# A two-layer hybrid diffusion block on one core: the second layer's modulation sums in the context feed-forward, norm scaling of queries and keys on ScalarE, mean squares of the latents by TensorE and one GpSimd power

## The chip, the cores and the metric

The kernel runs on one core of a Trainium2 chip, in one launch. The metric is the device time of one execution in microseconds (us), as the median of several. The engines are named as the profile does: PE (TensorE), PEld (its weight loads), DVE (VectorE), ACT (ScalarE), POOL (GpSimd) and SP, on whose queue all DMAs here are issued. Each engine executes its instructions in the order of its own stream.

## What is computed

A batch of one with 1024 latent tokens `x` and 256 context tokens `ctx`, width 1024, goes through two layers. Each layer has a mixer (layer 0 recurrent, layer 1 grouped-query attention with 8 query and 2 key heads of 128) and a gated feed-forward of 2816 with a convolution over tokens. Both are fed by a root-mean-square norm that is modulated by six vectors, which come from the condition `c` (for latents) or `c_ctx` (for context) by a product with `mod_w`:

```python
ml = _ada(c, mod_w[i], mod_b[i])          # six vectors of 1024: silu(c) @ w + b
mc = _ada(c_ctx[None], mod_w[i], mod_b[i])
h_l = _modulate(_rms(x), ml[0], ml[1])    # rms(x) * (1 + ml[1]) + ml[0]
...
x = x + ml[2] * mix_l
x = x + ml[5] * _conv_ffn(_modulate(_rms(x), ml[3], ml[4]), ffn_w_up[i], ffn_conv[i], ffn_w_down[i])
# _rms(x) = x * rsqrt(mean(x*x) + EPS)
# layer 1, queries and keys of each head: q = _rms(q) * q_norm; then a rotation (latents only)
```

The context's own output in layer 1 is not needed: there it gives keys and values only, so of `mc` of layer 1 just the shift and the scale of the mixer's input (indices 0 and 1) are used. The result is `_rms(x) * final_norm`.

## The kernel before

The latents are held transposed (features on partitions, tokens along the free axis) in two chunks of 512, `xT[1]` and `xT[2]`, and the context in `xT[0]`. Matmuls that matter for accuracy run as three passes over numbers split into a high and a low part (`mm3`, L155 to L157, with `split` at L160). A scheduler that simulates all engines sets the order of each engine's stream from the program's order, so moving code also moves the order of neighbouring instructions.

The stages, with their places in the profiled execution: the recurrent mixer of layer 0 (to 1020 us); its output projection `po` (L1292, 1020 to 1163 us), with the modulation vectors 0, 1 and 2 of layer 1 computed beside it; the context's feed-forward, `ffn_ctx` with its 22 steps of 128 features (`fg` L1206, `fd` L1215), beside which `ffn_prep` makes the latents' feed-forward input in pieces of 128 tokens (1163 to 1400 us); the latents' feed-forward of layer 0 (to 2105 us); the projections to values, keys and queries (2105 to 2325 us); attention and its output projection `apo` (to 2742 us), beside whose end `ffn_prep` runs again, for layer 1; the latents' feed-forward of layer 1 (to 3440 us); the last norm.

A modulation vector is made by `mod_steps`: for each of 8 blocks of 128 features a DMA loads a row block `mw` of `mod_w`, DVE multiplies it by the condition's scalar per partition and adds it into `macc` (L103), and at the end matmuls with a column of ones sum `macc` over partitions (`mps`, L229). For layer 1 this runs in blocks of 1024 columns beside `po` (24 loads of 512 KB), and in half blocks of 512 columns for indices 4, 3 and 5 in the key and query loops through `fill`, two steps per block of tokens (48 loads of 256 KB).

The norm of latents (`normalised`) squares a piece on ACT, sums over the 8 feature blocks on DVE with a TENSOR_REDUCE (L169), sums over partitions with a matmul that also transposes, so that the mean squares stand one per partition (`rm_cs`), raises that column to the power -1/2 on POOL (L176, 128x1 per 128 tokens), puts it on a diagonal (`rm_dg`) and multiplies by ones to spread it over all partitions (L180). `rms_mod` uses it for the input of the projections in four pieces of 256 tokens, `ffn_prep` in eight of 128.

In the projections, `proj` makes a block of 128 tokens by 256 columns with 24 matmuls (`qps`); there are 10 blocks for values (`v_proj`), 10 for keys and 32 for queries. `norm_rope` treats each key and query block: squares on ACT (`qsq`), TENSOR_REDUCE on DVE (`qss`, L1415), the power on POOL (`qrs`, 128x2, L1418), the scaling `qn<-qps,qrs` on DVE, the rotation with a table `tab` on DVE and POOL, and transposes on PE (`ktr`, `qtr`).

## Time and profile before

| | |
|---|---|
| median of 3 runs | 3487.37 us (3487.34 to 3493.24) |
| the profiled execution's own time | 3481.7 us |
| its span, first to last instruction | 3479.9 us |
| mean granted TensorE clock | 0.959 |
| PE busy | 3199.2 us, 92% of the span |
| DVE busy | 2385.0 us, 69% |
| POOL busy | 1579.2 us, 45% |
| ACT busy | 1277.4 us, 37% |
| DMA | 350 MB, mean 101 GB/s |

An engine's busy share is an average over stages with different limits. In the rows below, "idle before" is the time in which the engine had nothing to do ahead of the instructions of that row, with what ended most of it; a timeline row gives the start, the duration, the engine, the line and the tiles (out<-in).

### The profile page before, as it was taken

Reading aid. Unit: us, or ns where it says so; the run is one execution under the profiler, and the core shown is the slowest. Engines: PE = TensorE matmul, PEld = TensorE weight load, DVE = VectorE, ACT = ScalarE, POOL = GpSimd, SP = SyncE. Lnnn points to the kernel's source line nnn. Section 1 sums busy time; section 2 is a strip of 40 time slices with the busy share of each in tenths; the row PEclk is TensorE's granted clock in tenths of the full one; section 3 lists DMA queues with packets and bytes.
Section 4 is the critical chain, followed back from the end, with each engine's and each line's share of the span. In section 5 each row is a group of like instructions: output and inputs, shape, how many; then the busy total and the mean of one; then the engine's idle time right before and its main releaser. Section 6 shows DMA issues by size and latency. Waiting matters only on the chain.

```text
span 3479.9 us, 47261 instructions
## 1 busy us (share of the span) xinstructions
PE 3199.2 (92%) x16708; PEld 2676.1 (77%) x16708; DVE 2385.0 (69%) x3991; ACT 1277.4 (37%) x2772; POOL 1579.2 (45%) x1513
## 2 busy tenths in 40 slices
PE   7877988899979999799999997989999799999998
PEld 4766867687757888688788877878888677887877
DVE  5777365768857445677767677887657777767677
ACT  4423133654332122333333323236656433333333
POOL 2364463523304111565555543653433665655554
PEclk9988999999989999899999998999999899999999
DMA  5546455555476553211111122540110111111111
GB/s 186 151 119 170 130 148 147 151 156 174 153 258 215 146 152 118 77 58 44 52 58 49 58 67 72 160 141 25 37 55 28 37 50 42 52 58 49 58 49 73
DMA packets 446154, 350.12 MB, mean 101 GB/s; under 512 B 56756, under 2 KB 392862, under 8 KB 445150
## 3 DMA queue, kind: packets, MB, share of 16 engines
q1 hardware_dynamic: 445918, 347.10, 33.2%
q8 instruction: 132, 2.16, 0.3%
q14 instruction: 104, 0.85, 0.1%
HBM read 286.25 MB, written 60.76 MB: 100 GB/s over the span
## 4 chain that ended last, share of the span: by engine, by line
PE 41%; DVE 9%; POOL 3%; issue 2%; DMA 2%; ACT 2%; DVEq 0%; SPq 0%; POOLq 0%; ACTq 0%
PE fg L157 6%; PE fg L156 6%; PE fg L155 6%; PE fd L156 4%; PE fd L157 4%; PE fd L155 4%; PE apo L155 2%; DVE st L94 2%; PE apo L157 2%; PE apo L156 2%; PE apt L1521 2%; DMA mw<-in_mod_w_dram 2%; POOL w1l L94 1%; PE s L155 1%; DVE ft L103 1%
## 5 line engine op out<-in xcount | busy, mean ns | idle before, releaser
L103 DVE SCALAR_TENSOR_TENSOR xT<-fd,mod,xT 128x512 f32<-128x512 f32 (+1 forms) x432 | 291.1, 693 | 216.9 <-PE fd L157 176.8
L155 PE MATMUL pj<-hhi,whi 128*128 128x512 f32 (+1 forms) x696 | 263.2, 378 | 21.9 <-ACT raw L510 14.1
L103 DVE SCALAR_TENSOR_TENSOR macc<-mw,sc,macc 128x256 f32<-128x256 f32 (+2 forms) x301 | 231.6, 805 | 73.3 <-DMA mw<-in_mod_w_dram 71.7
L156 PE MATMUL fd<-gl,dh 128*128 128x512 f32 (+1 forms) x688 | 267.7, 389 | 7.1 <-DVE gl L94 7.1
L157 PE MATMUL fd<-gh,dl 128*128 128x512 f32 (+1 forms) x688 | 266.8, 388 | 0.0
L155 PE MATMUL fd<-gh,dh 128*128 128x512 f32 (+1 forms) x688 | 262.5, 392 | 1.6 <-ACT gh L1143 1.4
L156 PE MATMUL pj<-hlo,whi 128*128 128x512 f32 (+1 forms) x696 | 261.0, 375 | 0.7 <-DVE hlo L94 0.7
L157 PE MATMUL pj<-hhi,wlo 128*128 128x512 f32 (+1 forms) x696 | 260.5, 374 | 0.0
L94 DVE TENSOR_TENSOR st<-st 128x512 f32<-128x512 f32 x176 | 211.8, 1203 | 52.1 <-POOL s1l L94 34.1
L100 POOL TENSOR_SCALAR P<-P,rc 128x512 f32<-128x512 f32 (+1 forms) x192 | 116.7, 627 | 200.9 <-DVE rc L1507 59.7
L94 POOL TENSOR_TENSOR dl<-sd,dh 128x256 fp32r<-128x256 f32 x168 | 157.1, 950 | 109.1 <-ACT dh L160 107.1
L155 PEld LDWEIGHTS pj<-hhi,whi 128*128 128x128 f32 x696 | 138.5, 199 | 45.9 <-ACT raw L510 15.5
L94 POOL TENSOR_TENSOR w0l<-st,w0h 128x1024 fp32r<-128x1024 f32 x44 | 106.4, 2417 | 135.6 <-ACT w0h L1088 119.6
L94 POOL TENSOR_TENSOR p<-p,u 128x512 f32<-128x512 f32 (+1 forms) x45 | 93.0, 2067 | 156.8 <-DVE u L94 156.8
L156 PEld LDWEIGHTS fd<-gl,dh 128*128 128x128 f32 x688 | 129.9, 189 | 40.1 <-DVE gl L94 13.5
L1206 PE MATMUL fg<-hx,st 128*128 128x256 f32 x704 | 157.1, 379 | 0.0
L155 PEld LDWEIGHTS fd<-gh,dh 128*128 128x128 f32 x688 | 127.8, 188 | 36.6 <-ACT gh L1143 11.7
L155 PE MATMUL fg<-ah,w0h 128*128 128x512 f32 (+1 forms) x360 | 142.3, 396 | 14.6 <-ACT w0h L1088 8.9
L103 DVE SCALAR_TENSOR_TENSOR ft<-fraw,conv_f,ft 128x1024 f32<-128x1024 f32 x88 | 136.0, 1546 | 26.1 <-ACT ft L91 25.4
L156 PEld LDWEIGHTS pj<-hlo,whi 128*128 128x128 f32 x696 | 138.6, 199 | 19.4 <-DVE hlo L94 1.1
L157 PEld LDWEIGHTS pj<-hhi,wlo 128*128 128x128 f32 x696 | 138.2, 199 | 18.7 <-issue 0.2
L157 PEld LDWEIGHTS fd<-gh,dl 128*128 128x128 f32 x688 | 130.0, 189 | 26.3
(609 smaller groups left out, 9734.5 us busy)
## 6 DMA issues: line engine op xcount, KB each, us to landing
st<-in_ffn_w_up_dram SPq DMA_DIRECT2D x88, 512.0 KB
st<-in_ffn_w_up_dram SPq DMA_DIRECT2D x88, 256.0 KB
sd<-in_ffn_w_down_dram SPq DMA_DIRECT2D x176, 128.0 KB
sh<-sh_scr SPq DMA_DIRECT2D x80, 256.0 KB
mw<-in_mod_w_dram SPq DMA_DIRECT2D x128, 128.0 KB
wst<-in_rec_w_in_dram SPq DMA_DIRECT2D x56, 256.0 KB
st<-in_rec_w_out_dram SPq DMA_DIRECT2D x24, 512.0 KB
mw<-in_mod_w_dram SPq DMA_DIRECT2D x24, 512.0 KB
```

The lines of the kernel that those rows point to most:

```text
L94: e.tensor_tensor(out=o, in0=a, in1=b, op=op)
L100: e.tensor_scalar(out=o, in0=a, scalar1=s1, scalar2=s2, op0=op0, op1=op1)
L103: e.scalar_tensor_tensor(out=o, in0=a, scalar=s, in1=b, op0=op0, op1=op1)
L155: T.matmul(ps, lhsT=wh, rhs=xh, start=first, stop=False)
L156: T.matmul(ps, lhsT=wh, rhs=xl, start=False, stop=False)
L157: T.matmul(ps, lhsT=wl, rhs=xh, start=False, stop=last)
L1206: T.matmul(ps, lhsT=h[k // 4][:, k % 4], rhs=hx[:, k], start=k == 0, stop=k == KD - 1)
L1521: T.transpose(pt_[:, b], P[:, (b0 + b) * 128:(b0 + b + 1) * 128], ident)
```

## The change

It has three parts. First, the twelve half vectors of layer 1 are computed in the context's feed-forward, in the order 1, 0, 2, 4, 3, 5, all 512 wide, five steps behind each of the 22 steps; the pool of weight tiles there has 12 buffers in place of 14, and the context's keys are made ahead of the latents' norm. Second, a new function `normalised_pe` takes the place of `normalised` for the input of the projections (now in pieces of 128 tokens, each followed at once by its value block) and for `ffn_prep` of layer 1: PE sums the squares over feature blocks and partitions with eight matmuls against a 128x128 matrix of ones, so that the sums stand alike on all partitions, and POOL raises the whole 128x128 tile to -1/2. The mean's factor is moved into the modulation scale as sqrt(1024). Third, `norm_rope` sums squares by the accumulator output of ACT, scales by ACT with a per-partition scale, and has its factor sqrt(128) in the norm weights.

```diff
+    def normalised_pe(tmp, psp, tag, xs):
+        n = xs.shape[-1]
+        sq = tmp.tile([128, KD, n], F32, tag="rm_sq", name="rm_sq", bufs=5 if tmp.name.startswith("tmpe") else 2)
+        act(sq, xs, AF.Square)
+        ps = psp.tile([128, 512], F32, tag=tag, name="rm_ps")[:, 0:n]
+        for k in range(KD):
+            T.matmul(ps, lhsT=ones, rhs=sq[:, k], start=k == 0, stop=k == KD - 1)
+        r = tmp.tile([128, n], F32, tag="rm_rs", name="rm_rs", bufs=2)
+        ts(V, r, ps, D * EPS, None, ALU.add)
+        G.tensor_tensor(out=r, in0=r, in1=nhalf.to_broadcast([128, n]), op=ALU.pow)
+        return r[:, None, :].to_broadcast([128, KD, n]), sq
...
             if idx in (1, 4):
-                ts(V, m_, m_, 1.0, None, ALU.add)
+                if l == 1 and d == 0:
+                    ts(V, m_, m_, 1.0, D ** 0.5, ALU.add, ALU.mult)
+                else:
+                    ts(V, m_, m_, 1.0, None, ALU.add)
...
-                for idx in ((0,), (1,), (2,))[ci]:
-                    mod_acc(mp, pd, "d", 1, idx, (0, 1) if idx < 2 else (0,), 0, 1024)
...
-            fa.st = pool(pf, "fsta", 14)
+            fa.st = pool(pf, "fsta", 12)
+            mp = pool(pf, "mpa", 1)
+            mods = (None for i in (1, 0, 2, 4, 3, 5) for h in range(2)
+                    for _ in mod_steps(mp, pd, "d", 1, i, (0, 1) if i < 2 else (0,), h, 512))
...
             for f in range(NF):
                 step(f)
-                for _ in range((1, 0)[0] * (f >= (1, 0)[1])):
-                    next(prep, None)
+                next(prep, None)
+                for _ in range(5):
+                    next(mods, None)
...
-                    rms_mod(tmp, pd, "d", xT[ci], 512, mcol(1, 0, 1), mcol(1, 0, 0), hh[ci], hl[ci], w=256)
-                    for b in range(4 * ci - 2, 4 * ci + 2):
-                        v_proj(b)
+                    def done(p0, ci=ci):
+                        v_proj(4 * ci - 2 + p0 // 128)
+                    rms_mod(tmp, pd, "d", xT[ci], 512, mcol(1, 0, 1), mcol(1, 0, 0), hh[ci], hl[ci], w=128,
+                            norm=normalised_pe, done=done)
...
+            ts(V, nb_, nb_, 128 ** 0.5, None, ALU.mult)
...
-                act(sq, ps, AF.Square)
-                ss = qt_.tile([128, 2], F32, tag="ss", name="qss")
-                V.tensor_reduce(out=ss, in_=sq, axis=AX.X, op=ALU.add)
-                ts(V, ss, ss, 1.0 / 128, EPS, ALU.mult, ALU.add)
-                rs = qt_.tile([128, 2], F32, tag="rs", name="qrs")
-                G.tensor_tensor(out=rs, in0=ss, in1=nhalf.to_broadcast([128, 2]), op=ALU.pow)
+                ss = qt_.tile([128, 2, 2], F32, tag="ss", name="qss")
+                for h in range(2):
+                    S.activation(out=sq[:, h], in_=ps[:, h], func=AF.Square, accum_out=ss[:, 0, h:h + 1])
+                ts(V, ss[:, 0], ss[:, 0], 128 * EPS, None, ALU.add)
+                G.tensor_tensor(out=ss[:, 1], in0=ss[:, 0], in1=nhalf.to_broadcast([128, 2]), op=ALU.pow)
                 qn = qt_.tile([128, 2, 128], F32, tag="qn", name="qn")
-                tt(V, qn, ps, rs[:, :, None].to_broadcast([128, 2, 128]), ALU.mult)
+                for h in range(2):
+                    act(qn[:, h], ps[:, h], AF.Copy, scale=ss[:, 1, h:h + 1])
...
-            g1, g2 = (ffn_prep(1, ops, tmp, ci, 128) for ci in (1, 2))
+            g1, g2 = (ffn_prep(1, ops, tmp, ci, 128, normalised_pe) for ci in (1, 2))
```

POOL at the start of the projections, before (`rm_cs` are the latents' mean squares, `qwl` the low parts of the projection weights, `rm_sq` and `qhl` the modulated latents):

```order
L176 TENSOR_TENSOR rm_cs<-rm_cs,nhalf 128x2
L94 TENSOR_TENSOR qwl<-qws,qwh 128x1024
L176 TENSOR_TENSOR rm_cs<-rm_cs,nhalf 128x2
L94 TENSOR_TENSOR qwl<-qws,qwh 128x1024
L100 TENSOR_SCALAR rm_sq<-rm_sq,mod_73 128x256 x2
L94 TENSOR_TENSOR qwl<-qws,qwh 128x1024
L100 TENSOR_SCALAR rm_sq<-rm_sq,mod_73 128x256 x2
L94 TENSOR_TENSOR qhl_17360<-rm_sq,qhh_17357 128x2x256 x2
L176 TENSOR_TENSOR rm_cs<-rm_cs,nhalf 128x2 x2
L100 TENSOR_SCALAR rm_sq<-rm_sq,mod_73 128x256 x4
L94 TENSOR_TENSOR qhl_17361<-rm_sq,qhh_17358 128x2x256 x2
L94 TENSOR_TENSOR qwl<-qws,qwh 128x1024 x2
```

With the change the same place reads:

```order
L94 TENSOR_TENSOR qwl<-qws,qwh 128x1024 x4
L1420 TENSOR_TENSOR qss<-qss,nhalf 128x2 x2
L190 TENSOR_TENSOR rm_rs<-rm_rs,nhalf 128x128 x2
L100 TENSOR_SCALAR rm_sq<-rm_sq,mod_71 128x128 x4
L94 TENSOR_TENSOR qhl_17653<-rm_sq,qhh_17650 128x2x128 x2
```

The last three of these rows come four times in a row; the fourth time and what follows it are these rows of POOL:

```order
L190 TENSOR_TENSOR rm_rs<-rm_rs,nhalf 128x128 x2
L100 TENSOR_SCALAR rm_sq<-rm_sq,mod_71 128x128 x4
L94 TENSOR_TENSOR qhl_17654<-rm_sq,qhh_17651 128x2x128 x2
L94 TENSOR_TENSOR tab<-tab,nb 128x1024 x2
L94 TENSOR_TENSOR qwl<-qws,qwh 128x1024 x2
L1420 TENSOR_TENSOR qss<-qss,nhalf 128x2 x3
```

The powers of the keys' and queries' norms (128x2) of the latents stand behind all eight wide powers, and so do the table and the next weights.

POOL around the end of the output projection of attention (`awlo` are the low parts of its weights, `w0l` to `s3l` those of the first feed-forward step), before:

```order
L176 TENSOR_TENSOR rm_cs<-rm_cs,nhalf 128x1
L94 TENSOR_TENSOR awlo<-awst,awhi 128x1024 x2
L176 TENSOR_TENSOR rm_cs<-rm_cs,nhalf 128x1
L94 TENSOR_TENSOR s0l<-st,s0h 128x512
L176 TENSOR_TENSOR rm_cs<-rm_cs,nhalf 128x1
L94 TENSOR_TENSOR s2l<-st,s2h 128x512
L100 TENSOR_SCALAR rm_sq<-rm_sq,mod_73 128x128 x2
L94 TENSOR_TENSOR s1l<-st,s1h 128x512
L94 TENSOR_TENSOR awlo<-awst,awhi 128x1024
L176 TENSOR_TENSOR rm_cs<-rm_cs,nhalf 128x1
L94 TENSOR_TENSOR s3l<-st,s3h 128x512
```

And with the change:

```order
L94 TENSOR_TENSOR awlo<-awst,awhi 128x1024 x2
L190 TENSOR_TENSOR rm_rs<-rm_rs,nhalf 128x128
L94 TENSOR_TENSOR s0l<-st,s0h 128x512
L94 TENSOR_TENSOR s2l<-st,s2h 128x512
L190 TENSOR_TENSOR rm_rs<-rm_rs,nhalf 128x128
L94 TENSOR_TENSOR awlo<-awst,awhi 128x1024 x2
L100 TENSOR_SCALAR rm_sq<-rm_sq,mod_71 128x128 x2
L190 TENSOR_TENSOR rm_rs<-rm_rs,nhalf 128x128
L94 TENSOR_TENSOR s1l<-st,s1h 128x512
L100 TENSOR_SCALAR rm_sq<-rm_sq,mod_71 128x128 x2
L190 TENSOR_TENSOR rm_rs<-rm_rs,nhalf 128x128
L94 TENSOR_TENSOR awlo<-awst,awhi 128x1024 x2
```

Four wide powers now stand among the low parts of the projection's weights, two of them ahead of the third and fourth `awlo`, all four ahead of the fifth and sixth. The other four stand behind the rows shown.

SP in the context's feed-forward, before:

```order
L84 DMA mw<-in_mod_w_dram 128x1024 x5
L84 DMA st<-in_rec_w_out_dram 128x8x128
L84 DMA st<-in_ffn_w_up_dram 128x4x128 x18
L84 DMA st<-in_ffn_w_down_dram 128x512 x8
L84 DMA st<-in_ffn_w_up_dram 128x4x128 x16
```

With the change, where the loads of `mod_w` for layer 1 alternate with those of the feed-forward's weights:

```order
L84 DMA st<-in_ffn_w_up_dram 128x4x128
L84 DMA mw<-in_mod_w_dram 128x512 x7
L84 DMA st<-in_ffn_w_up_dram 128x4x128 x6
L84 DMA st<-in_ffn_w_down_dram 128x512 x2
L84 DMA mw<-in_mod_w_dram 128x512
L84 DMA st<-in_ffn_w_down_dram 128x512
L84 DMA mw<-in_mod_w_dram 128x512
L84 DMA st<-in_ffn_w_down_dram 128x512
```

The loads of `mod_w` left the stage ahead and the projections, and stand in this queue between the weights.

## Rows read from the trace of the kernel before

**Rows 1.** The page's part 1: busy time and share of the span of each engine.
```profile
PE 3199.2 (92%) x16708; PEld 2676.1 (77%) x16708; DVE 2385.0 (69%) x3991; ACT 1277.4 (37%) x2772; POOL 1579.2 (45%) x1513
```

**Rows 2.** The table of windows: stretch, its length, busy us of each engine, clock, DMA share, GB/s.
```profile
1020.00:1163.00 143.00, 133.17 (x597) 108.62 (x597) 96.25 (x101) 32.15 (x44) 45.17 (x22) 0.96 0.72 219
1163.00:1400.00 237.00, 232.67 (x1096) 204.80 (x1095) 122.83 (x219) 57.35 (x113) 30.94 (x36) 1.00 0.46 137
2150.00:2325.00 175.00, 151.88 (x1188) 148.12 (x1186) 139.29 (x306) 41.40 (x96) 108.09 (x135) 0.95 0.55 163
```

**Rows 3.** Costliest groups, POOL: the powers (nhalf) and one elementwise product, by form.
```profile
L1603 POOL TENSOR_TENSOR zst<-zst,nhalf 128x1 f32<-128x1 f32 x8 | 4.3, 550 | 22.0 <-DVE zst L100 22.0
...
L554 POOL TENSOR_TENSOR rr<-ssq,nhalf 128x10 f32<-128x10 f32 x4 | 8.0, 1999 | 12.0 <-DVE ssq L98 11.9
...
L94 POOL TENSOR_TENSOR tab<-tab,nb 128x1024 f32<-128x1024 f32 x4 | 10.1, 2559 | 2.2 <-DMA tab<-in_rope_dram 2.2
```

**Rows 4.** One tile's view: the powers of the queries' and keys' norms (qrs), min/median/max ns.
```profile
L1418 POOL TENSOR_TENSOR qrs<-qss,nhalf x42: 690/697/1065, 2170.8 to 2323.6; 128x2 f32<-128x2 f32 x42
```

**Rows 5.** Timeline of PE and groups, 1020 to 1163: sums of the modulation products.
```profile
1111.84 3.63 PE L229 MATMUL mps<-ones,macc 128*128 128x1 f32 x32
...
L103 DVE SCALAR_TENSOR_TENSOR macc<-mw,sc,macc 128x1024 f32<-128x1024 f32 x35 | 54.0, 1578 | 12.0 <-DMA mw<-in_mod_w_dram 11.9
```

**Rows 6.** Timeline of VectorE at the end of layer 0's feed-forward; then two windows there.
```profile
2089.58 3.71 DVE L169 TENSOR_REDUCE rm_rs<-rm_sq 128x256 f32<-128x2048 f32 x1
...
2097.00:2099.80 2.80, 1.27 (x10) 1.27 (x11) 2.51 (x5) 0.00 (x0) 0.00 (x0) 1.00 0.00 0
2099.90:2103.20 3.30, 3.30 (x17) 3.30 (x17) 1.28 (x4) 0.00 (x0) 0.00 (x0) 0.50 0.00 0
```

**Rows 7.** Timeline of POOL from the start of the projections.
```profile
2105.31 0.71 POOL L176 TENSOR_TENSOR rm_cs<-rm_cs,nhalf 128x2 f32<-128x2 f32 x1 [28.16 <-DVE rm_cs L100]
...
2119.97 3.00 POOL L94 TENSOR_TENSOR qhl<-rm_sq,qhh 128x512 fp32r<-128x512 f32 x2
2132.92 1.36 POOL L176 TENSOR_TENSOR rm_cs<-rm_cs,nhalf 128x2 f32<-128x2 f32 x2 [9.95 <-DVE rm_cs L100]
...
2156.14 4.77 POOL L94 TENSOR_TENSOR qwl<-qws,qwh 128x1024 fp32r<-128x1024 f32 x2 [8.76 <-ACT qwh L160]
2161.39 4.94 POOL L94 TENSOR_TENSOR tab<-tab,nb 128x1024 f32<-128x1024 f32 x2 [0.47 <-DMA tab<-in_rope_dram]
2170.80 1.36 POOL L1418 TENSOR_TENSOR qrs<-qss,nhalf 128x2 f32<-128x2 f32 x2 [4.47 <-DVE qss L100]
```

**Rows 8.** Timeline of PE: neighbouring projection matmuls; then groups of the stretch 2105 to 2325.
```profile
2154.10 0.28 PE L155 MATMUL qps<-qwh,qhh 128*128 128x256 f32 x1
2154.22 0.28 PE L156 MATMUL qps<-qwl,qhh 128*128 128x256 f32 x1
...
L103 DVE SCALAR_TENSOR_TENSOR macc<-mw,sc,macc 128x512 f32<-128x512 f32 x42 | 40.5, 965 | 15.1 <-DMA mw<-in_mod_w_dram 14.4 <-DVE qss L1415 0.3
...
L94 DVE TENSOR_TENSOR qn<-qps,qrs 128x256 f32<-128x256 f32 x42 | 17.2, 415 | 0.6 <-POOL qrs L1418 0.5
L1415 DVE TENSOR_REDUCE qss<-qsq 128x2 f32<-128x256 f32 x42 | 17.1, 409 | 2.8 <-ACT qsq L91 2.8
...
L1454 PE MATMUL qtr<-ident,qn 128*128 128x128 f32 x60 | 12.2, 286 | 11.5 <-DVE qss L100 5.6 <-DVE qn L94 5.4 <-DVE qh L94 0.4
```

**Rows 9.** Timeline of POOL around the end of the output projection.
```profile
2701.61 4.68 POOL L94 TENSOR_TENSOR awlo<-awst,awhi 128x1024 fp32r<-128x1024 f32 x2 [0.49 <-ACT awhi L160]
2706.24 1.02 POOL L176 TENSOR_TENSOR rm_cs<-rm_cs,nhalf 128x1 f32<-128x1 f32 x1
...
2732.07 2.40 POOL L94 TENSOR_TENSOR awlo<-awst,awhi 128x1024 fp32r<-128x1024 f32 x1 [1.97 <-ACT awhi L160]
2744.70 1.58 POOL L94 TENSOR_TENSOR rm_sq<-rm_sq 128x512 f32<-128x512 f32 x1 [10.23 <-DVE rm_sq L94]
...
2789.21 2.83 POOL L94 TENSOR_TENSOR w0l<-st,w0h 128x1024 fp32r<-128x1024 f32 x1
```

More of the change, by code (lines that the diff above doesn't have):

```diff
@@ L209, in rms_mod @@
                 modulate(sq, s1, sh, hi[:, :, p0:p0 + w], lo[:, :, p0:p0 + w])
+            if done is not None:
+                done(p0)
     def mod_steps(pool, psp, tag, l, idx, conds, part, width, bufs=2):
@@ L1251 @@
             wo = pool(po, "wo", 5)
-            mp = pool(po, "mpc", 1)
             mhl = {}
@@ L1320 @@
                 step(f)
-                for _ in range((1, 0)[0] * (f >= (1, 0)[1])):
-                    next(prep, None)
+                next(prep, None)
+                for _ in range(5):
+                    next(mods, None)
             for _ in prep:
+                pass
+            for _ in mods:
                 pass
@@ L1346 @@
             hp = {i: pool(pqq, f"hQ{i}", 1, side="right") for i in (2, 1, 0)}
-            wsp = pool(pqq, "qsp", 3)
+            wsp = pool(pqq, "qsp", 4)
             wst = pool(pqq, "qst", 2)
@@ L1377, in v_proj @@
                 tt(V, vl[:, b], ps, vh[:, b].bitcast(F32), ALU.subtract)
-            for b in range(2):
-                v_proj(b)
-            with ExitStack() as pt_q:
-                tmp = pool(pt_q, "tmpq", 2, side="right")
-                for ci in (1, 2):
-                    rms_mod(tmp, pd, "d", xT[ci], 512, mcol(1, 0, 1), mcol(1, 0, 0), hh[ci], hl[ci], w=256)
-                    for b in range(4 * ci - 2, 4 * ci + 2):
-                        v_proj(b)
-            rp = pool(pqq, "rp", 1, side="right")
-            qt_ = pool(pqq, "qt", 3)
-            mq = pool(pqq, "mq", 1)
-            mods = (None for i in (4, 3, 5) for h in range(2) for _ in mod_steps(mq, pd, "d", 1, i, (0,), h, 512))
-            def fill(n):
-                for _ in range(n):
-                    next(mods, None)
-            nb_ = rp.tile([128, 2, 2, 128], F32, name="nb")
+            qt_ = pool(pqq, "qt", 3)
+            nb_ = kvp.tile([128, 2, 2, 128], F32, name="nb")
             for a, src in ((0, att_q_norm), (1, att_k_norm)):
@@ L1432, in norm_rope, with k_proj @@
                 return qn
-            LAT = range(NB)
-            load_tab(1)
-            w = load_w(1024)
-            for b in LAT:
-                fill((0,2,1)[1])
-                kn = norm_rope(proj(w, b), b, 1)
+            wk = load_w(1024)
+            def k_proj(b):
+                kn = norm_rope(proj(wk, b), b, 1)
                 pt_ = pd.tile([128, 512], F32, tag="d", name="ktr")
@@ L1445 @@
                 tt(V, kTl[:, :, b * 128:(b + 1) * 128], pv, kTh[:, :, b * 128:(b + 1) * 128].bitcast(F32), ALU.subtract)
+            for b in range(2):
+                v_proj(b)
+            for b in range(2):
+                k_proj(b)
+            with ExitStack() as pt_q:
+                tmp = pool(pt_q, "tmpq", 1, side="right")
+                for ci in (1, 2):
+                    def done(p0, ci=ci):
+                        v_proj(4 * ci - 2 + p0 // 128)
+                    rms_mod(tmp, pd, "d", xT[ci], 512, mcol(1, 0, 1), mcol(1, 0, 0), hh[ci], hl[ci], w=128,
+                            norm=normalised_pe, done=done)
+            rp = pool(pqq, "rp", 1, side="right")
+            load_tab(1)
+            for b in range(2, NB):
+                k_proj(b)
             load_tab(0)
@@ L1449 @@
                 for b in range(2, NB):
-                    fill((0,2,1)[2])
                     qn = norm_rope(proj(w, b), b, 0)
@@ L1460 @@
                         dma(aq_scr[e, 2 * u:2 * u + 2, :, (b - 2) * 128:(b - 1) * 128].rearrange("h p t -> p h t"), qh[:, e])
-            for _ in mods:
-                pass
         if dbg is not None:
```

10 lines of the change are left out of this document (4 added, 6 removed).

## The prediction

> **What bounds the kernel now.** I read the page's busy times first, then the windows of the stages that the change touches, then the costliest groups and the timelines there. PE is busy 92% of the span [rows 1], so as a rule work taken from another engine buys nothing unless PE waits for it. The windows show where PE has slack [rows 2]: in the stage of the recurrent mixer's output projection it is busy 133.17 of 143 us, in the context's feed-forward 232.67 of 237 (PE-bound, DVE only 122.83), in the projections of layer 1 151.88 of 175, with DVE at 139.29. So the projections are the one stage where DVE's load matters. They make one power of 128x2 per block, the first at 2170.8 and the last at 2323.6 us [rows 4], 42 of them: 3.7 us a block, where PE's own part is 24 matmuls that start 0.12 us apart [rows 8], 2.88 us, and two transposes.
>
> **The price that decides: a power of 128x128 on POOL.** The trace has no power that wide. It has 128x1 at 0.550 us, 128x10 at 1.999 us [rows 3] and 128x2 at 0.697 us [rows 4]. From one column to two that is 0.147 us, from one to ten (1.999 - 0.550)/9 = 0.161 us per column: the price grows by the column, and 128 columns come to 0.697 + 126 x 0.147 = 19.2 us by the one slope and 0.550 + 127 x 0.161 = 21.0 us by the other. I take 20.5 us. The bound from below is the elementwise product of 128x1024 on the same engine, 2.559 us [rows 3], 2.5 ns per column: a power at that price would take 0.55 + 127 x 0.0025 = 0.87 us. I hold to the upper pair, because those rows are the same operation with the same broadcast exponent, and three widths lie on one line. The old form needed 0.55 to 0.70 us for the same tokens, since there the mean squares stood one per partition. The change has eight wide powers in the projections and eight in the preparation of layer 1's feed-forward: 16 x 20.5 = 328 us of POOL.
>
> The Trainium skill speaks the other way: "GPSIMD Engine Reference", section 3.1 (Elementwise — side-by-side cycle accounting), gives about 2.6 cycles per element for a two-input elementwise operation, which at its 1.2 GHz would be an estimated 0.28 us for 128 columns beside the dispatch; the sum would then be that of the first rival, 3441 us. The rows above do not agree for a power: 0.147 to 0.161 us per column is some 60 times the 2.5 ns of the product.
>
> **Part by part, on the scale of the profiled execution** (3481.7 us of its own time, span 3479.9; the median of the runs shown is 3487.4, 5.7 above).
>
> *Modulation sums leave the output projection's stage.* 24 loads of 512 KB go, 12.6 MB of the 143 us x 219 GB/s = 31 MB there [rows 2], and 80 rows of `mps` on PE, of which 32 took 3.63 us [rows 5]: 9 us. PE's idle time there is 143 - 133.17 = 10 us, part of it waits for weights that queue behind these loads. DVE's 35 products (1.578 us each) [rows 5] stand beside PE's work. I take -18, between -9 (PE's rows alone) and -19 (the idle time too).
>
> *They enter the context's feed-forward.* PE gets all 128 `mps` rows: 128 x 3.63/32 = 14.5 us on an engine that is already full [rows 2]. DVE gets 128 products of 128x512 at up to 0.965 us [rows 8], up to 124 us, so 247 us against 237 + 14: just under the bound, with the first six or seven steps over it. DMA gets 25 MB in addition to 237 x 137 = 32 MB, some 230 GB/s, which is about what the stage before it does now (219). SP now issues these loads between the feed-forward's weights; what would pay there is the weight behind a waiting `mw`, and the pool still holds 12. I take +18, between +14 and +44 (the rival below).
>
> *End of layer 0's feed-forward.* Two TENSOR_REDUCE of 3.7 us each, the first at 2089.58, sit on DVE among the additions that free PE's accumulators; after the pauses the granted clock is 0.50 from 2099.9 to 2103.2, that is the lower level, where it was 1.00 before [rows 6]. Both reductions go to PE: -5, bounds -7 and 0.
>
> *The projections.* DVE loses 48 products, a reduction (0.409) and a scaling (0.415) per block [rows 8]; ACT, with 41 of 175 us [rows 2], takes the latter two at no cost, since it has over 130 us to spare. That would leave PE as the bound. But in POOL's order the eight wide powers stand ahead of the table, the next weights and every power of a latent key or query. POOL is free at about 2120 us as now (its low parts of the first piece end at 2123) [rows 7]. Powers come in pairs of 41 us, because `rm_sq` has two buffers: the squares of the next pair wait for the low parts (`qhl`) of the pair before. Between pairs stand POOL's own products and low parts, casts, the value block that PE's order places ahead of the next eight sums, and those sums; the nearest row is the present pause between pieces, 9.95 us [rows 7]. I take 9. So the latents are ready at 2121 + 4 x 41 + 4 x 9 = 2321. The table and the next weights, 4.94 + 4.77 us [rows 7], follow: 2331. Of the 40 latent key and query blocks PE has about five made by then (the accumulators it has); the other 35 cost 2.88 us and two transposes of 0.14 to 0.286 us, some 3.3 us each: 115 us. With 5 us for the chain of the last block the last power is at about 2451 in place of 2323.6: +128. Bounds: +100 (19.2 us per power, pauses of 6) and +155 (21, pauses of 13). What is late next is attention's start, and it follows at once.
>
> *The preparation of layer 1's feed-forward.* Now POOL has `awlo` at 2701.61 and 2732.07, a power of 1.02 at 2706.24, and the last `w0l` at 2789.21 [rows 9]. With the change the first wide power starts at about 2706 and ends at 2727. The low parts of two weight tiles, 2.6 us, come next; the second power ends at 2750; `awlo` twice (4.7) and a product; the third ends at 2777; the fourth at 2800; the fifth and sixth `awlo`, which PE's output projection is waiting for, end at 2805. Now they end at 2734, so attention's output projection stands still for some 70 us. Two column blocks of its matmuls, some 11 us, then finish the second chunk, and only now can the last four powers start: 2818 + 4 x 21.5 = 2904, and with the last piece's products and the first weights `w0l` at 2917 in place of 2789: +128, bounds +95 (powers of 19.2, the first two behind attention) and +140. DVE's reductions that go (2 us a piece) are covered by the powers and give nothing.
>
> **Sum:** -18 + 18 - 5 + 128 + 128 = +251, so 3481.7 + 251 = 3733, and on the scale of the median 3738 us. A measurement can tell this kernel from no change from about 0.2%, 7 us, on.
>
> **Rivals.** First, a wide power costs as an elementwise product does (0.87 us). It decides as soon as 16 powers fit into POOL's idle time, below some 3 us each. Then the projections are PE-bound: 52 blocks x 2.88 = 150, 50 pairs of transposes at 0.42 = 21, sums of squares 14, together 185 in place of 218 (2105.4 to 2323.6): -33. The preparation gives back four reductions, -8, and the rest of the terms -5: -46, 3436, on the median's scale 3441 us, faster. For it: POOL's product of 1024 columns in 2.559 us. Against it: the three widths of the power on one line. Chance 0.08. Second, the line flattens beyond ten columns, say to 10 us: nearly all 16 powers are exposed, so 16 x 10.5 less, 160 or so in the places that wait: 3578. No row speaks for it. Chance 0.06. Third, the context's feed-forward becomes DVE-bound: in the first 6.4 steps DVE has 122.83/22 + 10 x 0.965 = 15.2 us per step against PE's 10.6, 30 us in all, and if none is made up later the term is +44: 3764. For it: DVE's sum is at the bound; against it: five products a step later, and accumulators and buffers that let PE run ahead. Chance 0.13. A change that does not do what it says would be one where the wide powers stood off the path, hidden beside attention and PE; POOL's order speaks against it.
>
> **Chances.** The forecast 0.73, the third rival 0.13, the second 0.06, the first 0.08, of which 0.01 for within 0.2%. The range is the bounds of the powers and of the third rival together: low 3481.7 + 5.7 - 19 + 14 - 7 + 100 + 95 = 3670, taken at 3655 for what overlaps that I don't see; high 3764 + 27 + 12 = 3803, taken at 3815. It leaves out the first two rivals and some tails. Faster 0.07, same 0.01, slower 0.92.
>
> **What would show it.** Right: POOL's L190 group at about 20 us each, 16 of them, POOL busy some 310 us more; eight of them between 2115 and 2320 with PE mostly idle between value blocks at a low granted clock; keys and queries at about 3.3 us a block; PE idle before `apo` for `awlo`. The first step falls if that group's mean is under 3 us; the third rival is shown by PE idle for DVE at `fd` between 1145 and 1400. A time under 3655 says that a power is cheaper or hidden, one above 3815 that the projections have a stall that I did not see.

## The result and the profile after

The changed kernel takes 3809.5 us (median of 4 runs, 3803.4 to 3812.2) against 3487.4 us beside it: 1.0925 of the time before, with a 95% interval of 1.0911 to 1.0939. (The 3487.4 are the median of three runs; a fourth took 7951.3 us and is left out.) That is slower by 322 us, where 251 were forecast, inside the range and near its upper end. The profiled execution took 3812.2 us, with a span of 3810.1.

The page's first part shows the mean of it, to be held against [rows 1]: POOL has 330 us more, PE 53 more, ACT 40 more and DVE 64 less, and PE's share falls since the span grew.

```profile
PE 3252.4 (85%) x16908; PEld 2702.0 (71%) x16908; DVE 2321.1 (61%) x3950; ACT 1317.0 (35%) x3010; POOL 1909.5 (50%) x1529
```

The first instruction of PE in each stage gives where the time went (us in the profiled execution; worked out from the traces' records):

| stage | before | after | change |
|---|---|---|---|
| mixer of layer 0, to the first `po` | 1020.5 | 1031.5 | +11.0 |
| output projection, to the first `fg` of the context | 142.9 | 127.0 | -16 |
| context's feed-forward, to the first `fg` of the latents | 248.9 | 283.9 | +35 |
| latents' feed-forward of layer 0 | 693.1 | 697.5 | +4 |
| projections, to the first score | 221.3 | 365.7 | +144 |
| from the first score to the first `apo` | 19.2 | 18.0 | -1 |
| rest of attention with its output projection, preparation and layer 1's feed-forward, to the last `fd` | 1120.1 | 1272.5 | +152 |

The mixer's 11 us are not the change's. In the twelve other kernels profiled in this study, whose work is the same up to there, that stage took 1023.9 to 1037.7 us; the one of before was the shortest.

The windows of the touched stages, with the columns of [rows 2]: length, busy time of PE, PEld, DVE, ACT and POOL, granted clock, DMA share, GB/s. They are the output projection, the context's feed-forward, the projections while the latents' norm runs, the key and query loop, and the preparation of layer 1's feed-forward.

```profile
1020.00:1158.00 138.00, 128.32 (x561) 104.52 (x561) 47.79 (x76) 35.73 (x48) 41.78 (x23) 0.97 0.54 161
1158.00:1437.00 279.00, 260.53 (x1218) 221.92 (x1217) 194.84 (x356) 54.80 (x110) 32.42 (x36) 0.97 0.66 197
2140.00:2380.00 240.00, 76.04 (x457) 71.08 (x457) 34.21 (x67) 39.03 (x86) 193.60 (x38) 0.62 0.05 15
2380.00:2505.00 125.00, 118.79 (x1002) 117.76 (x1000) 71.05 (x156) 65.97 (x282) 96.94 (x131) 1.00 0.40 117
2890.00:3130.00 240.00, 77.54 (x389) 65.97 (x387) 77.21 (x88) 46.00 (x85) 221.84 (x53) 0.64 0.04 11
```

In the third and the fifth, PE is busy for a third of the time and POOL for most of it. The granted clock there is 0.62 and 0.64, a mean of the two levels 0.50 and 1.00 (1.2 and 2.4 GHz): PE's work comes in short stretches between the waits for POOL and runs for a good part at the lower one (0.56 in 2212 to 2222 us, between the first two pairs of powers). In the fourth PE is busy 119 of 125 us at 1.00: the key and query loop is now bound by PE.

The groups of POOL's powers, by form, with mean ns:

```profile
L190 POOL TENSOR_TENSOR rm_rs<-rm_rs,nhalf 128x128 f32<-128x128 f32 x16 | 332.6, 20798 | 16.2 <-DVE rm_rs L98 16.2
L1420 POOL TENSOR_TENSOR qss<-qss,nhalf 128x2 f32<-128x2 f32 x42 | 30.7, 734 | 16.3 <-DVE qss L98 16.0
...
L174 POOL TENSOR_TENSOR rm_cs<-rm_cs,nhalf 128x1 f32<-128x1 f32 x12 | 6.7, 564 | 143.7 <-DVE rm_cs L100 143.7
```

The power that the trace of before could not show takes 20.8 us, 16 times; the powers of 128x1 and 128x2 take about what they took [rows 3, 4]. Ahead of the products that need these powers DVE stands idle for 254.7 us, waiting for them:

```profile
L94 DVE TENSOR_TENSOR rm_sq<-xT,rm_rs 128x1024 f32<-128x1024 f32 x16 | 28.5, 1781 | 254.7 <-POOL rm_rs L190 254.7
```

This is POOL's timeline in the projections:

```profile
2166.42 0.70 POOL L1420 TENSOR_TENSOR qss<-qss,nhalf 128x2 f32<-128x2 f32 x1 [0.59 <-DVE qss L98]
2170.93 41.41 POOL L190 TENSOR_TENSOR rm_rs<-rm_rs,nhalf 128x128 f32<-128x128 f32 x2 [3.80 <-DVE rm_rs L98]
...
2215.22 0.89 POOL L94 TENSOR_TENSOR qhl<-rm_sq,qhh 128x256 fp32r<-128x256 f32 x1
...
2221.95 41.40 POOL L190 TENSOR_TENSOR rm_rs<-rm_rs,nhalf 128x128 f32<-128x128 f32 x2 [3.80 <-DVE rm_rs L98]
...
2273.05 41.41 POOL L190 TENSOR_TENSOR rm_rs<-rm_rs,nhalf 128x128 f32<-128x128 f32 x2 [3.88 <-DVE rm_rs L98]
...
2324.20 41.41 POOL L190 TENSOR_TENSOR rm_rs<-rm_rs,nhalf 128x128 f32<-128x128 f32 x2 [3.92 <-DVE rm_rs L98]
...
2370.45 0.97 POOL L94 TENSOR_TENSOR qhl<-rm_sq,qhh 128x256 fp32r<-128x256 f32 x1 [1.07 <-ACT qhh L206]
2377.07 4.78 POOL L94 TENSOR_TENSOR tab<-tab,nb 128x1024 f32<-128x1024 f32 x2 [5.66 <-DMA tab<-in_rope_dram]
2381.83 4.74 POOL L94 TENSOR_TENSOR qwl<-qws,qwh 128x1024 fp32r<-128x1024 f32 x2
2386.53 2.02 POOL L1420 TENSOR_TENSOR qss<-qss,nhalf 128x2 f32<-128x2 f32 x3
```

Four pairs of 41.4 us, 51.1 us apart, then the table, the next weights and the first powers of latent keys: the order that was printed ahead of the prediction. POOL's timeline around the end of attention's output projection, for [rows 9]:

```profile
2878.75 5.14 POOL L94 TENSOR_TENSOR awlo<-awst,awhi 128x1024 fp32r<-128x1024 f32 x2 [1.77 <-ACT awhi L158]
2883.86 21.18 POOL L190 TENSOR_TENSOR rm_rs<-rm_rs,nhalf 128x128 f32<-128x128 f32 x1
...
2908.44 21.16 POOL L190 TENSOR_TENSOR rm_rs<-rm_rs,nhalf 128x128 f32<-128x128 f32 x1
2929.57 5.65 POOL L94 TENSOR_TENSOR awlo<-awst,awhi 128x1024 fp32r<-128x1024 f32 x2
...
2936.12 20.71 POOL L190 TENSOR_TENSOR rm_rs<-rm_rs,nhalf 128x128 f32<-128x128 f32 x1
...
2960.44 20.72 POOL L190 TENSOR_TENSOR rm_rs<-rm_rs,nhalf 128x128 f32<-128x128 f32 x1
2981.13 5.66 POOL L94 TENSOR_TENSOR awlo<-awst,awhi 128x1024 fp32r<-128x1024 f32 x2
...
2999.02 1.57 POOL L94 TENSOR_TENSOR rm_sq<-rm_sq 128x512 f32<-128x512 f32 x1 [9.20 <-DVE rm_sq L94]
...
3012.49 41.78 POOL L190 TENSOR_TENSOR rm_rs<-rm_rs,nhalf 128x128 f32<-128x128 f32 x2 [0.83 <-DVE rm_rs L98]
...
3056.84 20.72 POOL L190 TENSOR_TENSOR rm_rs<-rm_rs,nhalf 128x128 f32<-128x128 f32 x1
...
3079.59 20.72 POOL L190 TENSOR_TENSOR rm_rs<-rm_rs,nhalf 128x128 f32<-128x128 f32 x1
...
3114.86 2.41 POOL L94 TENSOR_TENSOR w0l<-st,w0h 128x1024 fp32r<-128x1024 f32 x1
```

The two `awlo` at 2981.13, for which PE waits, come behind four wide powers. PE waits 71.8 us for `awlo` in all. The first power of the second chunk starts at 3012.49, 16 us after the last `apo` (2996.3): products and low parts of the first chunk stand ahead of it in the orders of POOL and DVE.

### The profile page after: what moved, and what is told of

Same layout as the page of the kernel before. It is cut to its first block, busy times and chain, and to the rows that moved or that the text cites. A ratio compares the mean times of both kernels' runs of the same rounds, so it can differ in the third digit from the quotient of the medians.

```text
span 3810.1 us, 47892 instructions
## 1 busy us (share of the span) xinstructions
PE 3252.4 (85%) x16908; PEld 2702.0 (71%) x16908; DVE 2321.1 (61%) x3950; ACT 1317.0 (35%) x3010; POOL 1909.5 (50%) x1529
## 4 chain that ended last, share of the span: by engine, by line
PE 57%; DVE 15%; DMA 9%; POOL 8%; issue 7%; ACT 3%; SPq 1%; DVEq 0%; ACTq 0%; POOLq 0%
PE fg L155 6%; PE fg L154 6%; PE fg L153 6%; DMA mw<-in_mod_w_dram 5%; PE fd L154 4%; PE fd L155 4%; POOL rm_rs L190 4%; PE fd L153 4%; DVE macc L103 3%; PE apo L155 2%; PE apo L153 2%; PE apo L154 2%; PE apt L1535 2%; DVE st L94 2%; PE pj L153 2%
## 5 line engine op out<-in xcount | busy, mean ns | idle before, releaser
L190 POOL TENSOR_TENSOR rm_rs<-rm_rs,nhalf 128x128 f32<-128x128 f32 x16 | 332.6, 20798 | 16.2 <-DVE rm_rs L98 16.2
L103 DVE SCALAR_TENSOR_TENSOR macc<-mw,sc,macc 128x256 f32<-128x256 f32 (+1 forms) x336 | 220.8, 692 | 107.5 <-DMA mw<-in_mod_w_dram 106.2
L153 PE MATMUL qps<-qwh,qhh 128*128 128x256 f32 x416 | 125.9, 304 | 160.8 <-ACT qhh L206 149.7
L153 PEld LDWEIGHTS qps<-qwh,qhh 128*128 128x128 f32 x416 | 84.5, 204 | 163.2 <-ACT qhh L206 151.7
L94 DVE TENSOR_TENSOR rm_sq<-xT,rm_rs 128x1024 f32<-128x1024 f32 x16 | 28.5, 1781 | 254.7 <-POOL rm_rs L190 254.7
L1221 PE MATMUL fg<-hx,st 128*128 128x256 f32 x704 | 166.5, 389 | 5.0 <-DMA st<-in_ffn_w_up_dram 4.2
```

What stands on the lines that cost most here:

```text
L94: e.tensor_tensor(out=o, in0=a, in1=b, op=op)
L103: e.scalar_tensor_tensor(out=o, in0=a, scalar=s, in1=b, op0=op0, op1=op1)
L153: T.matmul(ps, lhsT=wh, rhs=xh, start=first, stop=False)
L190: G.tensor_tensor(out=r, in0=r, in1=nhalf.to_broadcast([128, n]), op=ALU.pow)
L1221: T.matmul(ps, lhsT=h[k // 4][:, k % 4], rhs=hx[:, k], start=k == 0, stop=k == KD - 1)
```

## The experiments

Twelve kernels were timed in all, the changed one among them. Their times, and the length of the three stages that matter, from the traces (us):

| kernel | median | ratio to before, 95% interval | context's feed-forward | projections | from the first `apo` to the last `fd` |
|---|---|---|---|---|---|
| before | 3487 | 1 | 248.9 | 221.3 | 1120.1 |
| after | 3809.5 | 1.0925 (1.0911 to 1.0939) | 283.9 | 365.7 | 1272.5 |
| narrow powers | 3534.9 | 1.0136 (1.0116 to 1.0156) | 283.4 | 234.4 | 1128.8 |
| key weights first | 3806.2 | 1.0917 (1.0898 to 1.0936) | 286.1 | 361.3 | 1271.4 |
| four buffers | 3792.9 | 1.0873 (1.0857 to 1.0889) | 269.4 | 365.1 | 1271.3 |
| sums moved alone | 3480.8 | 0.9978 (0.9964 to 0.9991) | 283.5 | 189.5 | 1122.1 |
| the same, wide powers in the preparation | 3626.6 | 1.0395 (1.0378 to 1.0412) | 286.3 | 188.5 | 1267.4 |
| third part alone | 3478.8 | 0.9975 (0.9963 to 0.9986) | 248.8 | 211.9 | 1121.9 |
| sums moved, four buffers, third part | 3466.2 | 0.9937 (0.9918 to 0.9957) | 268.6 | 187.3 | 1121.2 |
| half of the sums moved, third part | 3452.9 | 0.9898 (0.9881 to 0.9914) | 243.9 | 189.5 | 1122.1 |
| after with the old norm | 3522.9 | 1.0097 (1.0078 to 1.0116) | 286.0 | 223.7 | 1124.9 |
| narrow powers, old order | 3518.5 | 1.0086 (1.0062 to 1.0111) | 283.8 | 217.0 | 1129.1 |
| sums moved, four buffers, third part, pieces of 128 | 3477.6 | 0.9976 (0.9966 to 0.9986) | 266.9 | 204.4 | 1119.6 |

### The power made narrow

The idea of the second part is kept: PE still sums the squares. But the squares become the weights and a column of ones the moving operand, so that the sums stand one per partition.

```diff
-        ps = psp.tile([128, 512], F32, tag=tag, name="rm_ps")[:, 0:n]
-        for k in range(KD):
-            T.matmul(ps, lhsT=ones, rhs=sq[:, k], start=k == 0, stop=k == KD - 1)
...
-        G.tensor_tensor(out=r, in0=r, in1=nhalf.to_broadcast([128, n]), op=ALU.pow)
+        ps = psp.tile([128, 512], F32, tag=tag, name="rm_ps")
+        for k in range(KD):
+            T.matmul(ps[:, 0:1], lhsT=sq[:, k], rhs=ones[:, 0:1], start=k == 0, stop=k == KD - 1)
...
+        G.tensor_tensor(out=cs[:, 1:2], in0=cs[:, 0:1], in1=nhalf, op=ALU.pow)
+        dg = tmp.tile([128, n], F32, tag="rm_dg", name="rm_dg", bufs=2)
+        ts(V, dg, ident, cs[:, 1:2], None, ALU.mult)
+        T.matmul(ps[:, 256:256 + n], lhsT=ones, rhs=dg, start=True, stop=True)
```

> The changed kernel, but the squares are summed by TensorE with the piece's squares as weights against one column of ones, so that the 128 sums stand one per partition: the power is 128x1 and is spread by the diagonal and a second matmul, as before the change. Theory (the wide powers, 20.7 us each, are nearly the whole loss): the projections fall from 359 us in the changed kernel to about 200 us and the preparation of layer 1's feed-forward loses its 150 us, so about 3810 - 160 - 150 = 3500 us. Rival (the smaller pieces, the value blocks between them and the sums on TensorE cost by themselves): the time stays above 3600 us.

Measured: 3534.9 us. The same 16 powers are now this group of POOL:

```profile
L190 POOL TENSOR_TENSOR rm_cs<-rm_cs,nhalf 128x1 f32<-128x1 f32 x16 | 10.1, 632 | 44.2 <-DVE rm_cs L98 44.2
```

10 us in place of 333, and 275 us of time with them: the projections go from 366 to 234 us, the last stage from 1272 to 1129. The wide powers are most of the loss. But the projections stay 13 us above the kernel before and 45 above the one with the sums moved alone, so something of what the rival named costs too, though not as much as it said; the last three runs below take it up.

### One place of the two

```diff
-            g1, g2 = (ffn_prep(1, ops, tmp, ci, 128) for ci in (1, 2))
+            g1, g2 = (ffn_prep(1, ops, tmp, ci, 128, normalised_pe) for ci in (1, 2))
```

The scale sqrt(1024) goes into index 4 alone here.

> The kernel with the modulation sums moved (3480.8 us) and the wide powers in the preparation of layer 1's feed-forward alone, eight of them; the latents' input of the projections keeps its old norm. Theory (the two places pay separately, about 150 us each): 3481 + 150 = 3630 us, with attention's output projection ended some 75 us later and the feed-forward behind it some 75 more. Rival (part of the loss there was only the lateness of the projections): under 3600 us.

Measured: 3626.6 us, 146 above its base, as the theory had it. POOL's timeline in it:

```profile
2799.45 5.66 POOL L94 TENSOR_TENSOR awlo<-awst,awhi 128x1024 fp32r<-128x1024 f32 x2
...
2830.83 41.41 POOL L192 TENSOR_TENSOR rm_rs<-rm_rs,nhalf 128x128 f32<-128x128 f32 x2 [1.43 <-DVE rm_rs L98]
...
2932.83 2.40 POOL L94 TENSOR_TENSOR w0l<-st,w0h 128x1024 fp32r<-128x1024 f32 x1
```

The last `awlo` come at 2799, the fifth power starts 31 us later, the other three follow, and `w0l` at 2932.8. Counted from each kernel's own first `apo`, that `w0l` stands at 591.3 us here, at 591.3 in the changed kernel and at 443.3 in the kernel before. The two places pay separately.

### The sums moved alone

All of the first part, nothing else: both old places removed, the loop in the context's feed-forward as in the diff.

> The kernel before with the first part of the change alone: all modulation sums of layer 1 in the context's feed-forward, none beside the output projection or in the projections. Theory: the output projection's stage gains 14 us, the context's feed-forward loses about 35 us with the transition behind it, and the key and query loop gains 20 to 30 us, since DVE was its bound: 3485 us, within 10 of the kernel before. Rival (DVE was not the bound of that loop, or its norm chain takes the place): 3505 to 3515 us.

Measured: 3480.8 us, 0.22% faster, at the edge of what can be told. The terms are there: -13 in the output projection, +35 in the context's feed-forward, -32 in the projections. This is the key and query loop in it (same columns as above):

```profile
2185.00:2320.00 135.00, 129.96 (x1076) 127.93 (x1074) 99.32 (x246) 38.41 (x91) 101.37 (x137) 1.00 0.39 115
```

PE is busy 130 of 135 us at a granted clock of 1.00, without the third part of the change. So DVE's products, with their waits for loads, were what held that loop in the kernel before [rows 2, 8].

### What holds the context's feed-forward

DVE's and PE's waits there in the changed kernel, in us, times, and the longest:

```profile
DVE macc L103 <- DMA mw<-in_mod_w_dram: 51.9, 50, 3.7
...
PE mps L241 <- DVE macc L103: 9.2, 4, 5.6
```

DVE is busy 195 of 279 us and yet it is late: it stands still for 52 us, 50 times, for the next block of `mod_w`, of which two can be in flight, and its sums and the accumulations that free PE's tiles queue behind it. Of PE's idle time in these 279 us (18.5), 13.6 end with work of DVE, 9.2 of them at `mps`.

```diff
-            fa.st = pool(pf, "fsta", 12)
+            fa.st = pool(pf, "fsta", 10)
...
-                    for _ in mod_steps(mp, pd, "d", 1, i, (0, 1) if i < 2 else (0,), h, 512))
+                    for _ in mod_steps(mp, pd, "d", 1, i, (0, 1) if i < 2 else (0,), h, 512, 4))
```

> The changed kernel with four buffers in place of two for the blocks of mod_w in the context's feed-forward, paid for by two of the twelve weight buffers there. Theory: DVE waits 52 us for these blocks because only two are in flight, and TensorE waits behind DVE; with four the context's feed-forward falls by 15 to 20 us of its 279, to about 3790 us. Rival one (the stage is bound by TensorE's own added rows and DVE's work): no change. Rival two (the weights need their buffers): slower than 3812 us.

Measured: 3792.9 us, 16.6 less, and the stage 14.5 shorter. The wait in the same view:

```profile
DVE macc L103 <- DMA mw<-in_mod_w_dram: 17.2, 16, 3.3
```

A third of it is left; ten weight buffers were enough. The stage is still 20.5 us longer than in the kernel before, and PE's 128 rows of `mps` alone take 16 of them.

### The key weights first

SP's queue in the changed kernel before the first wide power:

```profile
2120.69 0.93 SPq L84 DMA_DIRECT2D qws<-in_att_w_qkv_dram  x2
2139.77 2.91 SPq L84 DMA_DIRECT2D nb<-in_att_q_norm_dram  x5
2142.73 2.33 SPq L84 DMA_DIRECT2D nb<-in_att_k_norm_dram  x5
2145.24 14.77 SPq L84 DMA_DIRECT2D qws<-in_att_w_qkv_dram  x4
```

The ten broadcasts of the norm weights (`nb`) start when layer 0's feed-forward has ended, and the loads of the key weights (`qws` from 2145) are behind them. The context's keys need these weights, PE's order has those keys ahead of the first sums of squares, and so the first wide power starts 31 us after the first value matmul.

```diff
+            wk = load_w(1024)
             nb_ = kvp.tile([128, 2, 2, 128], F32, name="nb")
...
-            wk = load_w(1024)
```

> The changed kernel with the load of the key weights written ahead of the ten broadcast loads of the norm weights. Theory: in the changed kernel the first wide power waits for the context's keys, whose weights' loads queue on SP behind the broadcasts, which wait for memory that layer 0's feed-forward frees at 2140 us; without that the first power starts some 15 us earlier after the end of that feed-forward and the whole time falls by 10 to 18 us, to about 3795 us. Rival (the weights wait for their own buffers, or something else arrives as late): no change, 3805 to 3812 us.

Measured: 3806.2 us: 3 less, inside the spread of the runs, so the expected 10 to 18 did not come. The first wide power starts 27.7 us after the first value matmul, in place of 31.0. SP's queue shows why:

```profile
2118.03 0.93 SPq L84 DMA_DIRECT2D qws<-in_att_w_qkv_dram  x2
2137.10 3.14 SPq L84 DMA_DIRECT2D nb<-in_att_q_norm_dram  x5
2140.28 0.90 SPq L84 DMA_DIRECT2D nb<-in_att_k_norm_dram  x2
2141.29 0.38 SPq L84 DMA_DIRECT2D qws<-in_att_w_qkv_dram  x1
2141.71 1.45 SPq L84 DMA_DIRECT2D nb<-in_att_k_norm_dram  x3
2143.26 10.86 SPq L84 DMA_DIRECT2D qws<-in_att_w_qkv_dram  x3
```

The scheduler put seven of the ten broadcasts ahead of the loads all the same, and the last loads are spread over 11 us: SP waits there for POOL's low parts of earlier weights (5.3 us) and for an earlier load (4.3 us), so that their buffers come free. In the changed kernel it waits for the same two (5.3 and 7.6 us), and issuing the ten broadcasts takes 5.5 us. So the rival holds for the most part: the key weights wait for their own buffers more than for the broadcasts. The edit did not take that wait away. A later kernel, the one of narrow powers with the old order, takes the keys themselves out of the way: there they stand behind the latents' norm, and the first power of POOL (128x1) is

```profile
2138.41 0.55 POOL L190 TENSOR_TENSOR rm_cs<-rm_cs,nhalf 128x1 f32<-128x1 f32 x1 [4.83 <-DVE rm_cs L98]
```

1.5 us before the first value matmul (2139.9). With narrow powers in the new order it starts 31.2 us after it. So the context's keys ahead of the sums hold the first power back by some 32 us; the forecast had it start 16 us after the first value matmul, for another reason (POOL's low parts).

### The third part alone

```diff
-                V.tensor_reduce(out=ss, in_=sq, axis=AX.X, op=ALU.add)
+                for h in range(2):
+                    S.activation(out=sq[:, h], in_=ps[:, h], func=AF.Square, accum_out=ss[:, 0, h:h + 1])
...
-                tt(V, qn, ps, rs[:, :, None].to_broadcast([128, 2, 128]), ALU.mult)
+                for h in range(2):
+                    act(qn[:, h], ps[:, h], AF.Copy, scale=ss[:, 1, h:h + 1])
```

> The kernel before with the third part alone: squares of keys and queries summed by ScalarE's accumulator and scaled by ScalarE. Theory (DVE bounds the key and query loop of the kernel before, so 0.8 us less of it per block counts in 40 blocks): 15 to 30 us less, 3457 to 3472 us. Rival (the loop waits for the loads of mod_w, not for DVE's own work, or the longer chain over ScalarE costs as much): 3480 to 3492 us.

Measured: 3478.8 us, 0.25% faster; the projections are 9 us shorter. That lies between theory and rival: with the sums still in the loop DVE is relieved by 0.8 us a block, but the waits for `mod_w` stay and grow (22.9 us between 2150 and 2330, where the kernel before has 14.4 between 2150 and 2325).

### Versions that beat both kernels

The third part and four buffers together with the sums moved, and the old norm of latents:

> The modulation sums moved, with four buffers for the blocks of mod_w and ten for the weights, the old norm of latents, and the third part (norms of queries and keys on ScalarE). Theory: 3480.8 less 13 for the four buffers, and a few us for the third part, since TensorE already bounds the key and query loop when the sums are gone: about 3465 us. Rival (the third part counts in full, some 25 us): 3445 us.

Measured: 3466.2 us. The projections are 187.3 us against 189.5 with the sums moved alone: the third part is worth at most 2 us once PE bounds the loop, as the theory had it. One trace each doesn't tell that from nothing: with the same projections as the sums moved alone the kernel with wide powers in the preparation has 188.5, and the next kernel, which has the third part, 189.5.

Then only the sums that stood in the projections were moved:

```diff
+            fa.st = pool(pf, "fsta", 12)
+            mp = pool(pf, "mpa", 1)
+            mods = (None for i in (4, 3, 5) for h in range(2)
+                    for _ in mod_steps(mp, pd, "d", 1, i, (0,), h, 512, 3))
...
+                for _ in range(3):
+                    next(mods, None)
```

> The kernel before with only the sums that stood in the projections (indices 4, 3, 5) moved to the context's feed-forward, at three steps behind each of its steps and with three buffers, the others left beside the output projection; with the third part and the old norm of latents. Theory: the output projection's stage stays as before, the context's feed-forward pays 48 of 128 rows of mps and half of the loads, some 10 us, and the projections gain 32 us: about 3463 us. Rival (moving all is better, since the output projection's stage gives back 14): above 3470 us.

Measured: 3452.9 us, 1.0% under the kernel before and the best of the study. The window of the context's feed-forward with the transition:

```profile
1173.00:1417.00 244.00, 238.78 (x1144) 210.47 (x1144) 150.22 (x271) 56.94 (x113) 32.81 (x36) 1.00 0.59 176
```

PE is busy 239 of 244 us; the stage is no longer than before (249), where 10 us more were expected. DVE has 48 of the 128 products here, half of the loads and three buffers, and no wait of PE for its sums shows; which of the three does it was not tried apart. The stage is 5 us shorter than before, with PE idle for 5.6 us in place of 14.2; why is not shown.

### What is left in the projections

Three runs take apart why narrow powers leave the projections at 234 us, where the sums moved alone give 189.

The old norm in the new order (`norm=normalised_pe` taken out in both places, and the scale):

> The changed kernel with the old norm of latents in both places (DVE's reduction, the transposing sum, the power of 128x1), everything else as changed: pieces of 128 tokens, value blocks between them, the context's keys first. With narrow powers and sums on TensorE that version took 3534.9 us, some 57 more than the sums moved and the third part should. Theory (the order costs it: the value block that TensorE has ahead of each next piece's sums, and the context's keys that wait for their weights): it stays near 3530 us, with the projections at some 230 us. Rival (the sums on TensorE cost it): 3485 to 3495 us, with the projections near 190.

The narrow powers in the old order:

```diff
-            for b in range(2):
-                k_proj(b)
...
-                    def done(p0, ci=ci):
-                        v_proj(4 * ci - 2 + p0 // 128)
...
+                    for b in range(4 * ci - 2, 4 * ci + 2):
+                        v_proj(b)
...
+            wk = load_w(1024)
+            for b in range(NB):
+                k_proj(b)
```

> The kernel with the narrow powers and the sums on TensorE (3534.9 us), with the old order in the projections: value blocks behind each whole chunk, the context's keys with the others behind the latents' norm, their weights loaded there. Theory (the order costs): the projections fall from 234 us to 190 to 200, so some 3495 us. Rival (the sums on TensorE cost): no change, 3530 to 3540 us.

And the piece's width alone:

```diff
-                    rms_mod(tmp, pd, "d", xT[ci], 512, mcol(1, 0, 1), mcol(1, 0, 0), hh[ci], hl[ci], w=256)
+                    rms_mod(tmp, pd, "d", xT[ci], 512, mcol(1, 0, 1), mcol(1, 0, 0), hh[ci], hl[ci], w=128)
```

> The kernel of 3466.2 us (sums moved with four buffers, third part, old norm and old order) with one edit: the latents' norm in the projections in eight pieces of 128 tokens in place of four of 256, in the same two buffers of squares. Theory (the smaller pieces cost: only 256 tokens are in flight, so the pieces go one pair after the other): the latents are ready some 25 us later and the time is 3485 to 3497 us. Rival (the width of a piece is indifferent; the other new things in the projections cost): 3463 to 3470 us.

Measured: 3522.9, 3518.5 and 3477.6 us. The first lies near its theory (3530 us) and far from its rival, so the order costs; the other two lie between theory and rival, so neither held alone there. In the projections, three pairs of kernels differ in one thing: pieces of 128 in place of 256 lengthen the projections from 187.3 to 204.4 us (+17, with 11 in the medians); the new order, with narrow powers, from 217.0 to 234.4 (+17); the sums on PE, in the new order, from 223.7 to 234.4 (+11). From 204.4 to 217.0 (sums on PE, old order) and to 223.7 (old norm, new order) the pools of the weights' low parts and of the norm weights change as well. Wide powers add 131 to the 234.4.

The sums on PE were to relieve DVE, and PE pays for them. All matmuls of the latents' norm (`rm_ps`) together keep PE busy for 23.6 us with the narrow sums in the new order, of which 128 matmuls with one column of ones are 18.8, and for 6.7 us with the old norm; in the old order for 20.8 and 6.5. That is 17 and 14 us more, on an engine that is busy for most of the stage, where the stages are 11 and 13 longer. For the new order, half of the cost shows as one wait: PE stands 9 us for the context's key weights (`qwh`) in both kernels that have it.

## Why the prediction was right, and where it was off

**The price of the wide power: right.** 20.8 us were measured for 20.5 taken. Its step from 128x1 is (20.80 - 0.55)/127 = 0.159 us per column, between the two slopes of [rows 3, 4]. The first rival (0.87 us) and the second (10 us) are out. The rule of the Trainium skill's "GPSIMD Engine Reference", section 3.1, on two-input elementwise operations does not price a power: the one of 128 columns was measured at 74 times the estimated 0.28 us.

**The projections: right in mechanism, 16 us short of the measured +144.** The first power starts 31 us after the first value matmul, where 16 were taken. That start is the mis-sized term: I let POOL be free and overlooked that PE has the context's keys ahead of the first sums, with weights that come late on SP, behind ten broadcasts and for want of buffers. The rest nearly cancels: the pairs are 51.1 us apart where 50 were taken and the table waits 5.7 us for its load, together 6 us more up to the first latent key's power, and from there to the last power it takes 117 us, where 120 were taken.

**The preparation: right in mechanism, 24 us short of the measured +152,** which lies beyond its upper bound of +140. The first half came as forecast: PE waits 71.8 us for `awlo`, where some 70 were taken. The second half is short: the fifth power starts 16 us after the last `apo`, where the working has 2 (2805 + 11, then 2818). That pause isn't new. In the kernel before, the power behind the last `apo` (to 2742.0) starts at 2757.9, also 16 us later, a row of its trace that [rows 9] doesn't have. The last `apo` itself (+77 for +74) and the pauses between the last powers add 3 us each, and slower matmuls behind them 4 (last section).

**The context's feed-forward: +35 for +18.** The third rival's size came closer (+44), but not its mechanism: it had DVE's own work as the bound, and DVE was busy 195 of 279 us. Its sign, PE idle for DVE at `fd`, shows 2.6 us. DVE waits for blocks of `mod_w`, two in flight; I had named the weights as what would be late on that queue, and not the products' own blocks. Four buffers gave 14.5 us back. PE's 128 rows keep it busy for 16.6 us, where 14.5 were taken.

**The output projection's stage: right,** -16 for -18, and -13 with the sums moved alone.

**The end of layer 0's feed-forward: -5 forecast, +4 measured,** outside its bounds. The reductions went, and with them the stall: PE's idle time in that stage falls from 15.8 to 10.3 us. But PE's busy time there rises by 10 us, a term that the forecast has at nothing; the last section tells where.

**The key and query loop: right for the wrong half.** PE became the bound as forecast, but by the products' leaving; the scaling on ACT is worth 9 us alone and at most 2 behind the move.

**The first rival's sum** counts 50 pairs of transposes, where the trace of before has 42 key and query blocks: 3 us too much, in a rival that is out.

Of the 330 us between the two profiled spans 11 are the mixer's spread; the terms that were too small by 16, 24, 17, 9 and 2 make up the rest of the 79 us between them and the 251. All of them erred to the same side. That the time still lies in the range is in part luck: its upper end of 3815 carries 26 us for the third rival, which did not come as it was described.

## What to carry to other kernels

A power on POOL was paid by the column here, from 1 to 128 of them: put the values one per partition before it, even if a diagonal and a matmul must spread them again. Before work is moved into a stage, count what is in flight there as well as the busy times: two buffers under a stream of loads made an engine late that was busy 70% of the time. And read an order row by row to the instruction that matters: of the two terms that came out short in POOL's stages, one stood in the printed order (the two powers of the context's keys ahead of the first wide one) and the other, the 16 us behind the last `apo`, in the trace of the kernel before, and neither was priced.
